# A two-layer hybrid backbone in fp32 pairs: where the vector work of the seven-product SwiGLU stands

## The chip, the cores and the metric

The kernel runs on one core of one Trainium2 chip. The metric is device microseconds for one execution of the whole program. TensorE (PE in the profile, with its weight loads as PEld) does the matmuls, VectorE (DVE), ScalarE (ACT) and GpSimd (POOL) do the element-wise work, and the SP queue issues nearly all transfers; GpSimd issues a few of its own.

## The reference

Two layers work on 512 latent tokens and 256 context tokens of width 1024. A layer is a half-weighted SwiGLU, a token mixer, and another half-weighted SwiGLU; each is modulated beforehand (shift, scale), gated, and closed by a LayerNorm.

```python
def swiglu(u, w_in, w_out):                 # w_in 1024 x 5632, w_out 2816 x 1024
    a, v = jnp.split(u @ w_in, 2, axis=-1)
    return (jax.nn.silu(a) * v) @ w_out

def ffn_sublayer(h, shift, scale, gate, w_in, w_out, g, b):
    y = swiglu(modulate(h, shift, scale), w_in, w_out)
    return layer_norm(ALPHA * h + FFN_RES * gate * y, g, b)
```

Mixer 0 is neighbourhood attention over a grid with all context keys beside it, mixer 1 a windowed attention with rotary positions and a sink. The shifts, scales and gates of a layer come from `silu(c) @ w_mod + b_mod`, one set for latent tokens and one for context tokens. Context tokens go through the same weights, except that the last layer drops them after its mixer has used them.

## The kernel before

Activations lie with the feature on the partitions: eight tiles of 128 x 768 (512 latent and 256 context tokens). Every product is made of fp32r pairs: a value is split into a high part and the rest, so one product is three matmuls (`mm3`, lines 145 to 148). Weights come in units of four raw quarters of 128 x 512. `split_w` (L102, L104) casts the high part on ScalarE and takes the rest on GpSimd; a variant (L106, L107) gets the rest from a transfer that GpSimd issues and that adds to what lies there. The pairs go into a ring of eight, or, on request, into the twelve "slab" tiles of the phase that the mixers use. Five raw buffers feed all of it.

There are four SwiGLU calls, named 0a, 0b, 1a and 1b in the tiles' names. `ffn` cuts the 2816 hidden columns into 11 chunks `ci` of 256, that is two blocks `i` of 128.

- An ordinary chunk: `av` makes the two products of a block for one group of tokens (48 matmuls into `pa` and `pv`), then silu, a multiplication, a cast to `gh` and the rest to `gl`. `down` multiplies with the output weights, six matmuls per output tile `pd`, and `accumulate` (L427) adds the gated result to the residual `z`.
- A seven-product chunk (0a from `ci` 3, 0b and 1a from `ci` 2, in each case to `ci` 8; none in 1b): `seven` computes the two products of a block with a Strassen-like scheme, seven products of 12 matmuls with 384 columns. `quarters` forms the four sums of weight quarters (`S`, L538: two on VectorE, two on GpSimd) and splits seven operands. `sums` formed the matching sums of activations once per call (`x`, `T`, L487 to L509), and `fourth` one more. The output sums (L567) add the seven results, in SBUF tiles `y`, and make `gh` and `gl`. The `down` of such a chunk is held back until the first `seven` of the next chunk has been emitted.

Beside that runs the modulation vector of later sub-layers: `gemv_dve` makes a list of steps, each a multiply-and-reduce on VectorE (L198, tile `jk`) of one transposed weight tile (`wt` in two buffers, or `zspare`, L195). `tick` emits steps at a pace that spreads them over the chunks, and `behind` keeps each step after the VectorE instruction that `last` names; it does not keep it ahead of anything. In 0a there are 192 steps, in 0b 96, in 1a 128, of which the last 64 use each weight tile once and all others twice.

The order on each engine is made by the Tile framework's planner from its own cost estimates, instruction by instruction, by program order where several are ready. Each engine then takes its list strictly in that order, and so does the SP queue.

In chunk 0 of 0b and 1b the LayerNorm of the last token groups is not finished when the chunk starts (`apart`, lines 665 to 672): the first group is computed and sent down, and then the chunk's three weight units are read, cast and split a second time for the remaining groups.

Of the kernel before, what the change touches and what calls it, by code (L numbers as in the profile page):

```python
# [8 lines left out]
F32 = mybir.dt.float32  # L9
# [29 lines left out]
def hybrid_kernel(ctx: ExitStack, tc: tile.TileContext, h0, cc, crow, wmod, wmodt, bmod, lnp, wst,  # L39
# [391 lines left out]
    def ffn(nm, groups, gt, mid, post, units=(), opened={}, head=None, apart=None):  # L431
# [7 lines left out]
        def av(w, f, g, gh, gl, ps=None, k0=0):  # L439
            c0, c1, st = g  # L440
            n = c1 - c0
            if ps:
                pa, pv = ps
            else:
                pa = bank("mm", f"pa{nm}_{f}_{c0}")
                mmk(pa[:, :n], w, 0, c0, c1, k0)
                pv = bank("c", f"pv{nm}_{f}_{c0}")
                mmk(pv[:, :n], w, P, c0, c1, k0)
            sl = t2(f"sl{nm}_{f}_{c0}", "sl")
            nc.scalar.activation(sl[:, :n], pa[:, :n], AF.Silu)  # L450
            nc.vector.tensor_tensor(out=sl[:, :n], in0=pv[:, :n], in1=sl[:, :n], op=ALU.mult)
            nc.scalar.copy(gh[:, c0:c1], sl[:, :n])
            nc.vector.tensor_tensor(out=gl[:, c0:c1], in0=sl[:, :n], in1=gh[:, c0:c1].bitcast(F32), op=ALU.subtract)

        turn = [0]

        def next_bank(nm):
            turn[0] += 1
            return bank(("mm", "s", "c")[turn[0] % 3], nm)

        def down(w, ci, gs, g, ticks):
            c0, c1, st = g
            for d in range(DT):
                pn = f"pd{nm}_{ci}_{c0}_{d}"
                pd = (next_bank(pn) if ticks else bank("sst"[d % 3], pn))[:, :c1 - c0]
                for i in range(2):
                    mm3(pd, rw(w, i, d * P, (d + 1) * P), [t[:, c0:c1] for t in gs[i]], i == 0, i == 1)
                accumulate(pd, d, c0, c1, st, gts[0])
                if ticks:
                    tick()  # L470

        gts = []
        nb = groups[-1][1] // 256
# [56 lines left out]
        def quarters(u):  # L530

            src = wst[u].rearrange("p (k c) -> p k c", c=256)
            a11, a12, a21, a22 = [raw_quarter(src[:, h * 4:h * 4 + 4, m * P:m * P + P], f"{u}_{m}{h}")
                                  for m in range(2) for h in range(2)]

            def tt(eng, n, a, b, o):
                t = t2(f"S{u}_{n}")
                eng.tensor_tensor(out=t[:], in0=a[:], in1=b[:], op=o)  # L538
                return t

            def pair(n, src):
                hi, lo = ring_pair(f"{u}_{n}")
                split_w(hi, lo, src)
                return hi, lo

            out = [pair("a11", a11), pair("a12", a12)]
            s1 = tt(nc.vector, 1, a21, a22, ALU.add)
            s2 = tt(nc.vector, 2, s1, a11, ALU.subtract)
            out += [pair("s2", s2), pair("s1", s1)]
            s4 = tt(nc.gpsimd, 4, a12, s2, ALU.subtract)  # L550
            s3 = tt(nc.gpsimd, 3, a11, a21, ALU.subtract)
            return out + [pair("s4", s4), pair("s3", s3), pair("a22", a22)]

        def seven(un, u, gh, gl):

            w = quarters(u)
            plain = [[[half(t[h4 * 4 + k], h) for t in (uh, ul)] for k in range(4)] for h4, h in ((0, 0), (1, 0), (1, 1), (0, 1))]
            b11, b21, b22, x4 = plain

            def product(n, b):  # L560
                ps = next_bank(f"p{n}{un}")
                for k in range(4):
                    mm3(as_half(ps[:, 0:n2]), [t[:, k * P:(k + 1) * P] for t in w[n]], b[k], k == 0, k == 3)
                return ps[:, 0:n2]

            def op(out, x, y, o=ALU.add, eng=nc.vector):
                i = eng.tensor_tensor(out=out, in0=x, in1=y, op=o)  # L567
                if eng is nc.vector:
                    last[0] = i
                return i  # L570
# [12 lines left out]
            tick()  # L583
            op(sb, product(4, b22), sb)
            nc.scalar.activation(sb, sb, AF.Silu)
            tick()
            op(va, product(5, ts[2]), va)
            op(vb, va, vb)
            tick()
            op(va, va, product(6, x4), ALU.subtract)  # L590
            for h, (v, x) in enumerate(((vb, sb), (va, sa))):
                op(v, v, x, ALU.mult)
                nc.scalar.copy(half(gh, 1 - h), as_half(v))
# [5 lines left out]
        gts.append(gt())  # L599
        late_downs = []  # L600
        s0 = NCH if nb == 2 else 3 if opened else 2
        weight = [0] + [2.2] * (s0 - 1) + [1.0] * (NCH - 2 - s0)
        each = sum(n + 1 for n, _ in bg) / (sum(weight) - 0.1)
        for ci in list(range(NCH)) + [("r", NCH - 2)]:
            r = isinstance(ci, tuple)
            if not r and 0 < ci < NCH - 2 and nb > 2:
                phase("T")
                pace[0] = each * weight[ci] / (2 * DT if ci < s0 else 2 * DT + 14)
                if ci == s0 - 1:
                    saved = sums()  # L610
            if not r and s0 <= ci < NCH - 2:
# [21 lines left out]
                continue  # L633
            if ci == NCH - 2:
                phase("S")
            i0 = wpos[0]
            late = ci == NCH - 2
            if late:
                again = i0
# [667 lines left out]
```

## Time and profile before

| | |
|---|---|
| Time, median of 3 runs | 2940.4 us (2936.29 to 2943.12) |
| The profiled execution | 2943.35 us |
| Its span | 2941.6 us |
| PE busy | 2759.2 us (94%) |
| VectorE busy | 1868.6 us (64%) |
| GpSimd busy | 1609.7 us (55%) |
| ScalarE busy | 1206.0 us (41%) |
| Transferred | 319.07 MB, mean 108 GB/s |

How to read it: a row of a group names line, engine, operation, output and inputs with buffer numbers left out, then busy time and the mean duration of one in nanoseconds, then the idle time of the engine ahead of them and what ended it. A row of waits gives the microseconds in total, the number of times and the longest. A row of a stretch of time gives the stretch, its length, and the busy time of PE, PEld, VectorE, ScalarE and GpSimd with the number of instructions, then the granted clock of TensorE, the share of the transfer engines' time that was used, and GB/s. A row of the timeline begins with start and duration in microseconds, and ends, in brackets, with the idle time ahead of it and what ended that.

### The profile page before, as it was taken

The numbers are of one execution on the slowest core, as the hardware profiler recorded it, in microseconds if no ns is written. First come the engines' busy times: TensorE is split into PE (matmuls) and PEld (weight loads), VectorE is DVE, ScalarE is ACT, GpSimd is POOL, SyncE is SP. The second block draws the span as 40 slices with busy tenths as digits, with TensorE's granted clock in tenths as the row PEclk, the third lists the DMA queues.
The fourth block names the chain that finished last, engine by engine and source line by source line (L and its number), as shares of the span: only waits on it lengthen the run. The fifth ranks groups of instructions, "written<-read, shape, count | busy, mean of one in ns | idle before, by whom it ended". The sixth has DMA issues, their size and how long they took to land. (4 is left out here: it accounts for less than half of the span.)

```text
span 2941.6 us, 48796 instructions
## 1 busy us (share of the span) xinstructions
PE 2759.2 (94%) x17626; PEld 2479.4 (84%) x17626; DVE 1868.6 (64%) x4024; ACT 1206.0 (41%) x2460; POOL 1609.7 (55%) x1410
## 2 busy tenths in 40 slices
PE   8999999989999978999999799999997999899997
PEld 5788888888888867898998688989886777799997
DVE  3698777385555687765664977675648667733335
ACT  4223433266445453343433423434335655523233
POOL 4646554465434567665645766565446544744453
PEclk9999999999999989999999999999999999899998
DMA  8456555232211222545452325556522111333332
GB/s 298 133 159 175 131 138 157 84 89 80 66 55 52 69 81 77 140 112 125 113 149 77 92 80 158 136 166 160 160 84 61 52 40 30 90 91 93 100 111 75
DMA packets 259443, 319.07 MB, mean 108 GB/s; under 512 B 28160, under 2 KB 140928, under 8 KB 258176
## 3 DMA queue, kind: packets, MB, share of 16 engines
q1 hardware_dynamic: 247392, 294.83, 33.7%
q0 software_dynamic: 11520, 20.98, 4.2%
q8 instruction: 139, 2.28, 0.3%
q14 instruction: 104, 0.85, 0.1%
q10 hardware_dynamic: 288, 0.14, 0.0%
HBM read 309.05 MB, written 11.20 MB: 109 GB/s over the span
## 5 line engine op out<-in xcount | busy, mean ns | idle before, releaser
L104 POOL TENSOR_TENSOR wl<-wr,wh 128x512 fp32r<-128x512 f32 x392 | 517.9, 1339 | 425.3 <-ACT wh L102 322.4
L102 ACT CAST wh<-wr 128x512 fp32r<-128x512 f32 x392 | 239.0, 619 | 256.6 <-DMA wr<-in_wst_dram 44.1
L104 POOL TENSOR_TENSOR wl_s<-S,wh_s 128x512 fp32r<-128x512 f32 x160 | 218.5, 1374 | 92.0 <-ACT wh_s L102 91.7
L102 ACT CAST wh_s<-S 128x512 fp32r<-128x512 f32 x160 | 97.3, 619 | 270.8 <-DVE S L538 49.5
L104 POOL TENSOR_TENSOR wl_a<-wr,wh_a 128x512 fp32r<-128x512 f32 x120 | 160.1, 1338 | 72.9 <-ACT wh_a L102 67.7
L198 DVE CUSTOM_DVE_ANT_0 jk<-wt,cb 128x512 f32<-128x512 f32 x278 | 185.4, 678 | 7.2 <-ACT cb L211 3.8
L538 POOL TENSOR_TENSOR S<-wr,S 128x512 f32<-128x512 f32 x40 | 52.7, 1317 | 157.2 <-DVE S L538 92.4
L427 DVE SCALAR_TENSOR_TENSOR z<-pd0b,gt,z 128x256 f32<-128x256 f32 (+1 forms) x176 | 99.4, 597 | 30.4 <-PE pd0b L148 30.4
L102 ACT CAST wh_a<-wr 128x512 fp32r<-128x512 f32 x120 | 74.5, 620 | 103.4 <-POOL wl_a L104 15.4
L427 DVE SCALAR_TENSOR_TENSOR z<-pd0a,gt,z 128x512 f32<-128x512 f32 (+1 forms) x168 | 98.7, 617 | 27.3 <-PE pd0a L148 27.3
L427 DVE SCALAR_TENSOR_TENSOR z<-pd1a,gt,z 128x512 f32<-128x512 f32 (+1 forms) x168 | 98.1, 616 | 26.2 <-PE pd1a L148 26.2
L427 DVE SCALAR_TENSOR_TENSOR z<-pd1b,gt,z 128x256 f32<-128x256 f32 x147 | 69.4, 481 | 71.3 <-PE pd1b L148 69.5
L761 POOL TENSOR_SCALAR p<-p,l 128x512 f32<-128x512 f32 x64 | 44.8, 701 | 119.0 <-DVE l L859 110.9
L538 DVE TENSOR_TENSOR S<-wr,wr 128x512 f32<-128x512 f32 x40 | 29.4, 735 | 112.8 <-DMA wr<-in_wst_dram 112.8
L198 DVE CUSTOM_DVE_ANT_0 jk<-zspare,cb 128x512 f32<-128x512 f32 x138 | 92.6, 678 | 7.0 <-DMA zspare<-in_wmodt_dram 6.1
L305 POOL TENSOR_SCALAR z<-z,ag_None,ab_None 128x256 f32<-128x256 f32 (+1 forms) x78 | 72.0, 931 | 38.8 <-DVE uh L291 29.9
L146 PE MATMUL pa1b<-uh,wh 128*128 128x256 f32 x320 | 91.3, 285 | 0.5 <-DVE uh L291 0.5
L148 PE MATMUL pa1b<-uh,wl 128*128 128x256 f32 x320 | 91.1, 285 | 0.0
L146 PE MATMUL pv1b<-uh,wh 128*128 128x256 f32 x320 | 91.1, 285 | 0.0
L147 PE MATMUL pa1b<-ul,wh 128*128 128x256 f32 x320 | 91.1, 285 | 0.0
L147 PE MATMUL pv1b<-ul,wh 128*128 128x256 f32 x320 | 90.9, 284 | 0.0
L148 PE MATMUL pv1b<-uh,wl 128*128 128x256 f32 x320 | 90.9, 284 | 0.0
(1406 smaller groups left out, 10711.5 us busy)
## 6 DMA issues: line engine op xcount, KB each, us to landing
wr<-in_wst_dram SPq DMA_DIRECT2D x552, 256.0 KB
wt<-in_wmodt_dram SPq DMA_DIRECT2D x160, 256.0 KB
zspare<-in_wmodt_dram SPq DMA_DIRECT2D x80, 256.0 KB
wr_0b<-in_wst_dram SPq DMA_DIRECT2D x41, 256.0 KB
wr_1b<-in_wst_dram SPq DMA_DIRECT2D x41, 256.0 KB
wr_2b<-in_wst_dram SPq DMA_DIRECT2D x41, 256.0 KB
wr_3b<-in_wst_dram SPq DMA_DIRECT2D x41, 256.0 KB
wm<-in_wmod_dram SPq DMA_DIRECT2D x8, 1024.0 KB
```

The lines of the kernel that those rows point to most:

```text
L102: nc.scalar.copy(hi[:], src[:])
L104: nc.gpsimd.tensor_tensor(out=lo[:], in0=src[:], in1=hi[:].bitcast(F32), op=ALU.subtract)
L146: nc.tensor.matmul(ps, a[0], b[0], start=first, stop=False)
L147: nc.tensor.matmul(ps, a[0], b[1], start=False, stop=False)
L148: nc.tensor.matmul(ps, a[1], b[0], start=False, stop=last)
L198: x = nc.vector.tensor_tensor_reduce(out=junk[:], in0=w[:], in1=cb[st], scale=1.0, scalar=0.0, op0=ALU.mult, op1=ALU.add, accum_out=acc[:, ...
L305: nc.gpsimd.tensor_scalar(out=zs, in0=zs, scalar1=prm[2][:, d:d + 1], scalar2=prm[3][:, d:d + 1], op0=ALU.mult, op1=ALU.add)
L427: last[0] = nc.vector.scalar_tensor_tensor(out=zt(d, c0, c1), in0=pd, scalar=gt[:, d, st:st + 1], in1=zt(d, c0, c1), op0=ALU.mult, op1=ALU ...
L538: eng.tensor_tensor(out=t[:], in0=a[:], in1=b[:], op=o)
L761: nc.gpsimd.tensor_scalar(out=p, in0=p, scalar1=r, scalar2=0.0, op0=ALU.mult, op1=ALU.add)
```

## The change

1. *Output sums.* In `av` the product is written back into the PSUM bank `pv`, and `gh` and `gl` are made from there. In `seven`, result 3 is added straight from its bank by VectorE (it had been copied by ScalarE and added by GpSimd), and the last additions, the multiplications and the rests are done in the banks of products 5 and 6. So each VectorE operation there has at least one operand in PSUM. The upper half is finished right behind product 5.
2. *Weight sums.* All four sums `S` are on GpSimd.
3. *Steps.* `tick` is no longer called in `down`. It is called once behind each `av` of the chunks between 0 and the first seven-product chunk (four times per chunk), and, as before, behind each product of `seven` (14 times per chunk). The paces follow: an early chunk has the weight 1.6 instead of 2.2. `av` now sets `last` too.
4. *Reloads.* In chunk 0 of 0b and 1b the third unit (the output weights) goes into slabs, the first two stay in the ring, and nothing is read again.

```diff
@@ av
-            nc.vector.tensor_tensor(out=sl[:, :n], in0=pv[:, :n], in1=sl[:, :n], op=ALU.mult)
-            nc.scalar.copy(gh[:, c0:c1], sl[:, :n])
-            nc.vector.tensor_tensor(out=gl[:, c0:c1], in0=sl[:, :n], in1=gh[:, c0:c1].bitcast(F32), op=ALU.subtract)
+            last[0] = nc.vector.tensor_tensor(out=pv[:, :n], in0=pv[:, :n], in1=sl[:, :n], op=ALU.mult)
+            nc.scalar.copy(gh[:, c0:c1], pv[:, :n])
+            nc.vector.tensor_tensor(out=gl[:, c0:c1], in0=pv[:, :n], in1=gh[:, c0:c1].bitcast(F32), op=ALU.subtract)
@@ down
                 accumulate(pd, d, c0, c1, st, gts[0])
-                if ticks:
-                    tick()
@@ quarters
-            s1 = tt(nc.vector, 1, a21, a22, ALU.add)
-            s2 = tt(nc.vector, 2, s1, a11, ALU.subtract)
+            s1 = tt(1, a21, a22, ALU.add)
+            s2 = tt(2, s1, a11, ALU.subtract)
@@ seven
+            def finish(v, x, h):
+                op(v, v, x, ALU.mult)
+                nc.scalar.copy(half(gh, h), as_half(v))
+                op(half(gl, h), as_half(v), half(gh, h).bitcast(F32), ALU.subtract)
...
-            nc.scalar.copy(vb, product(3, ts[0]))
-            op(sb, va, vb, eng=nc.gpsimd)
+            op(vb, product(3, ts[0]), va)
             tick()
-            op(sb, product(4, b22), sb)
+            op(sb, product(4, b22), vb)
             nc.scalar.activation(sb, sb, AF.Silu)
             tick()
-            op(va, product(5, ts[2]), va)
-            op(vb, va, vb)
+            x = product(5, ts[2])
+            op(va, x, va)
+            op(x, x, vb)
+            finish(x, sb, 1)
             tick()
-            op(va, va, product(6, x4), ALU.subtract)
-            for h, (v, x) in enumerate(((vb, sb), (va, sa))):
-                op(v, v, x, ALU.mult)
-                nc.scalar.copy(half(gh, 1 - h), as_half(v))
-                op(half(gl, 1 - h), as_half(v), half(gh, 1 - h).bitcast(F32), ALU.subtract)
+            x = product(6, x4)
+            op(x, va, x, ALU.subtract)
+            finish(x, sa, 0)
             tick()
@@ the chunks
-        weight = [0] + [2.2] * (s0 - 1) + [1.0] * (NCH - 2 - s0)
+        weight = [0] + [1.6] * (s0 - 1) + [1.0] * (NCH - 2 - s0)
...
-                pace[0] = each * weight[ci] / (2 * DT if ci < s0 else 2 * DT + 14)
+                pace[0] = each * weight[ci] / (4 if ci < s0 else 14)
...
-            w = [wunit(again=again + i) if r else unit(ci == NCH - 1 and i == 2) for i in range(3)]
+            w = [wunit(again=again + i) if r else unit(i == 2 and (ci == NCH - 1 or ci == 0 and apart is not None)) for i in range(3)]
...
                     av(w[i], f"{cn}_{i}", g, *gs[i], opened.get((i, g)) if ci == 0 else None, 4 if late else 0)
+                    if nb > 2 and not r and 0 < ci < s0:
+                        tick()
...
                 dn(head[0])
-                w = [wunit(again=i0 + i) for i in range(3)]
                 avs(*[(g, i) for g in head[1:] for i in range(2)])
```

More of the change, by code (lines that the diff above doesn't have):

```diff
@@ L459, in next_bank, with down @@
             return bank(("mm", "s", "c")[turn[0] % 3], nm)
-        def down(w, ci, gs, g, ticks):
+        def down(w, ci, gs, g, spread):
             c0, c1, st = g
@@ L464, in down @@
                 pn = f"pd{nm}_{ci}_{c0}_{d}"
-                pd = (next_bank(pn) if ticks else bank("sst"[d % 3], pn))[:, :c1 - c0]
+                pd = (next_bank(pn) if spread else bank("sst"[d % 3], pn))[:, :c1 - c0]
                 for i in range(2):
@@ L534, in quarters, with tt @@
                                   for m in range(2) for h in range(2)]
-            def tt(eng, n, a, b, o):
+            def tt(n, a, b, o):
                 t = t2(f"S{u}_{n}")
-                eng.tensor_tensor(out=t[:], in0=a[:], in1=b[:], op=o)
+                nc.gpsimd.tensor_tensor(out=t[:], in0=a[:], in1=b[:], op=o)
                 return t
@@ L546, in quarters @@
             out = [pair("a11", a11), pair("a12", a12)]
-            s1 = tt(nc.vector, 1, a21, a22, ALU.add)
-            s2 = tt(nc.vector, 2, s1, a11, ALU.subtract)
+            s1 = tt(1, a21, a22, ALU.add)
+            s2 = tt(2, s1, a11, ALU.subtract)
             out += [pair("s2", s2), pair("s1", s1)]
-            s4 = tt(nc.gpsimd, 4, a12, s2, ALU.subtract)
-            s3 = tt(nc.gpsimd, 3, a11, a21, ALU.subtract)
+            s4 = tt(4, a12, s2, ALU.subtract)
+            s3 = tt(3, a11, a21, ALU.subtract)
             return out + [pair("s4", s4), pair("s3", s3), pair("a22", a22)]
@@ L564, in product, with op @@
                 return ps[:, 0:n2]
[L566 to L570, printed above, removed]
+            def op(out, x, y, o=ALU.add):
+                last[0] = nc.vector.tensor_tensor(out=out, in0=x, in1=y, op=o)
+            def finish(v, x, h):
+                op(v, v, x, ALU.mult)
+                nc.scalar.copy(half(gh, h), as_half(v))
+                op(half(gl, h), as_half(v), half(gh, h).bitcast(F32), ALU.subtract)
             sa, sb = [t2(f"y{un}_{i}", "sl")[:, 0:n2] for i in range(2)]
@@ L635, in ffn @@
                 phase("S")
-            i0 = wpos[0]
             late = ci == NCH - 2
             if late:
-                again = i0
-            w = [wunit(again=again + i) if r else unit(ci == NCH - 1 and i == 2) for i in range(3)]
+                again = wpos[0]
+            w = [wunit(again=again + i) if r else unit(i == 2 and (ci == NCH - 1 or ci == 0 and apart is not None)) for i in range(3)]
             cn = f"r{ci[1]}" if r else f"{ci}"
```

## The prediction

> **What bounds the kernel now.** I read the page first, then the stretches of the seven-product chunks one by one, then who waits for whom there, then the order of single instructions.
>
> ```profile
> span 2941.6 us, 48796 instructions
> PE 2759.2 (94%) x17626; PEld 2479.4 (84%) x17626; DVE 1868.6 (64%) x4024; ACT 1206.0 (41%) x2460; POOL 1609.7 (55%) x1410
> ```
>
> The profiled run took 2943.35 us, 1.75 beyond its span and 3 above the median 2940.4. TensorE is the bound, so the change can only win time in which TensorE does not issue. Each row below runs from the first seven-product matmul of a SwiGLU (0a, 0b, 1a) to the first of its last such product group.
>
> ```profile
> 213.10:484.70 271.60, 254.68 (x1415) 235.64 (x1414) 212.65 (x466) 100.90 (x187) 159.64 (x130) 1.00 0.54 145
> 1194.50:1499.20 304.70, 296.50 (x1679) 280.91 (x1678) 195.96 (x413) 120.50 (x221) 187.34 (x154) 0.99 0.47 123
> 1760.30:2080.20 319.90, 303.19 (x1679) 283.15 (x1678) 219.66 (x479) 120.64 (x223) 188.17 (x154) 0.98 0.57 154
> ```
>
> A busy PE row overstates, because records overlap; start-to-start is the true price:
>
> ```profile
> 289.03 0.34 PE L147 MATMUL p20a<-T0a_3l,wh_s 128*128 128x384 f32 x1
> 290.07 0.34 PE L147 MATMUL p30a<-T0a_1l,wh_s 128*128 128x384 f32 x1
> 148.91 0.39 PE L147 MATMUL pd0a<-gl0a,wh 128*128 128x512 f32 x1
> 149.83 0.39 PE L148 MATMUL pd0a<-gh0a,wl 128*128 128x512 f32 x1
> 152.23 0.28 PE L147 MATMUL pd0a<-gl0a,wh 128*128 128x256 f32 x1
> 152.70 0.28 PE L148 MATMUL pd0a<-gh0a,wl 128*128 128x256 f32 x1
> ```
>
> Six steps make 1.04 us at 384 columns (0.173 each), four make 0.92 at 512 (0.23) and 0.47 at 256 (0.1175). A seven() is 84 matmuls, 14.6 us; a down() over both groups 48 x 0.23 + 48 x 0.1175 = 16.7 us; a chunk of two sevens and one down 45.8 us. The stretches hold 11, 13 and 13 sevens and 5, 6 and 6 downs: 243.7, 289.5 and 289.5 us, plus some 1.9 us each for the 11 matmuls above that count. What TensorE loses is thus about **26, 13 and 28.5 us, together 68**.
>
> ```profile
> PE pd0a L146 <- DVE z L427: 22.5, 28, 3.6
> PE pd1a L146 <- DVE z L427: 10.3, 20, 1.7
> PE pd1a L146 <- DVE y1a L567: 8.4, 3, 4.2
> PE pd0b L146 <- DVE z L427: 8.0, 13, 1.7
> ...
> DVE S L538 <- DMA wr<-in_wst_dram: 112.8, 19, 9.6
> DVE y0b L567 <- POOL y0b L567: 49.0, 13, 4.4
> ```
>
> TensorE waits in down() for banks that VectorE has not emptied, and VectorE itself stands waiting: for raw weights that a sum needs, and for a Pool addition inside seven(). One such chain:
>
> ```profile
> 313.27 0.69 DVE L538 TENSOR_TENSOR S<-wr,wr 128x512 f32<-128x512 f32 x1 [7.94 <-DMA wr<-in_wst_dram]
> 314.61 0.55 DVE L567 TENSOR_TENSOR y0a<-p40a,y0a 128x384 f32<-128x384 f32 x1
> 322.36 0.74 DVE L427 SCALAR_TENSOR_TENSOR z<-pd0a,gt,z 128x512 f32<-128x512 f32 x1
> ...
> 323.15 0.50 PE L146 MATMUL pd0a<-gh0a,wh_3b 128*128 128x512 f32 x1 [1.65 <-DVE z L427]
> ...
> 299.80:312.30 12.50, 12.50 (x74) 12.50 (x73) 4.39 (x11) 6.18 (x12) 5.45 (x6) 1.00 0.90 194
> 312.30:335.00 22.70, 19.11 (x99) 14.71 (x98) 21.45 (x40) 4.45 (x8) 13.12 (x10) 1.00 0.30 93
> ```
>
> VectorE's queue is in order: one sum waits 7.94 us for its transfer, products 4 to 6 stay in their banks, and the next down takes 22.7 us instead of 16.7. The price of that one wait is 6 us.
>
> **The change part by part.** Durations used:
>
> ```profile
> L567 DVE TENSOR_TENSOR y10a<-y00a,y10a 128x384 f32<-128x384 f32 x12 | 16.7, 1390 | 1.0
> L567 DVE TENSOR_TENSOR y00b<-p20b,y00b x14: 554/558/559, 1201.2 to 1504.1; 128x384 f32<-128x384 f32 x14
> L567 POOL TENSOR_TENSOR y0b<-y00b,y10b 128x384 f32<-128x384 f32 x14 | 14.8, 1057 | 0.0
> L538 DVE TENSOR_TENSOR S<-wr,wr 128x512 f32<-128x512 f32 x40 | 29.4, 735 | 112.8 <-DMA wr<-in_wst_dram 112.8
> L538 POOL TENSOR_TENSOR S<-wr,S 128x512 f32<-128x512 f32 x40 | 52.7, 1317 | 157.2 <-DVE S L538 92.4 <-issue 53.2 <-DMA cb<-in_crow_dram 6.5
> L198 DVE CUSTOM_DVE_ANT_0 jk<-wt,cb 128x512 f32<-128x512 f32 x278 | 185.4, 678 | 7.2 <-ACT cb L211 3.8 <-DMA wt<-in_wmodt_dram 2.8
> L107 POOL DMA_DIRECT2D wl_0b<-in_wst_dram x20 | 17.8, 892 | 39.6 <-ACT wl_0b L106 12.3 <-ACT gh0b L593 10.5 <-ACT gh1a L593 8.1
> ```
>
> *Sums with a PSUM operand.* Per seven, VectorE had ten operations, five of them with both inputs in SBUF, where the same shape averages up to 1.39 us instead of 0.558. It will have eleven at 0.558, 6.1 us. The Pool addition (1.06) and one ScalarE copy go; the wait of 49 us in 0b and its like in 0a and 1a have no cause left. Banks of products 5 and 6 and of pv are held 2 to 3 us longer; the next user of such a bank comes six products (12.5 us) or one av later, so I cost that at nothing; without that distance it would be 2 to 3 us per seven.
> The Trainium skill, page "SBUF — State Buffer", section "Who interferes with whom", says a VectorE instruction with two SBUF inputs is shut out while a GpSimd instruction reads SBUF. The 1.39 against 0.558 us agrees.
>
> *Weight sums on Pool.* VectorE loses 40 x 2 sums and the 112.8 us in which it stood for their transfers. Pool gains 80 x 1.32 us and loses 40 x 1.06, +1.6 us per seven; it works 11 x 1.32 = 14.5 us per seven and 4 x 0.89 for the transfers it issues, 32.6 of 45.8 us per chunk. Now Pool's head waits for raw weights; behind it stand the low parts (L104) and the accumulating transfers (L107), and TensorE after them. The lead:
>
> ```profile
> 318.87 3.15 POOL L104 TENSOR_TENSOR wl_s<-S,wh_s 128x512 fp32r<-128x512 f32 x2
> 339.13 0.33 PE L146 MATMUL p20a<-T0a_0h,wh_s 128*128 128x384 f32 x1
> ```
>
> The low part ends at 322.0 and is read at 339.1: 17 us. Two sums on Pool take 2.6 us of it, and TensorE's own 6 us of delay goes: 8 us remain. Cost zero; with the lead gone, 2.6 us per seven.
> The Trainium skill, page "GPSIMD Engine Reference", section "4.1 Engine selection", speaks against this part: an elementwise sum belongs on VectorE, GpSimd being about twice as slow. The two L538 rows agree (1317 against 735 ns); by that rule the change would lose, which is the second rival.
>
> *Steps beside products alone.* The 416 steps are the same in number. In 0a a seven-chunk gets 193/9.1 = 21.2 of them in 14 ticks instead of 18.7 in 30, so 10.6 per seven: 7.2 us, with 6.1 above 13.3 of 14.6. Then down() has only its accumulations:
>
> ```profile
> L427 DVE SCALAR_TENSOR_TENSOR z<-pd0a,gt,z 128x512 f32<-128x512 f32 x88 | 63.5, 743 | 24.0 <-PE pd0a L148 24.0
> L427 DVE SCALAR_TENSOR_TENSOR z<-pd0a,gt,z 128x256 f32<-128x256 f32 x80 | 35.5, 478 | 3.3 <-PE pd0a L148 3.3
> ...
> PE pd0a L146 <- DVE z L427: 3.4, 4, 1.5
> ```
>
> 8 x 0.743 + 8 x 0.478 = 9.8 of 16.7 us: VectorE has room to catch up. The last row is 180 to 240 us, the down of 0a's chunk 2, where steps stood between accumulations; with 0b's and 1a's chunk 1 I take 5 us back.
> The steps' transfers move too and meet the weights' (DMA share 0.90 above, raws waited for 8 us). Three tiles in flight with 8 us are some 5 per seven. 0a needs 5.3, 0b (11.4 steps per chunk, two per tile) 2.9, and 1a 3.8, but 7.7 once its last 64 steps use a tile each. There steps come late and VectorE stands for wt instead of wr. I leave a loss of 7 us in 0a, 4 in 0b and 12 in 1a; bounds are 0 and the 68 as now. **Gain: 68 - 23 = 45.**
>
> *Fewer reloads.* 24 transfers, casts and low parts go in 0b and 1b.
>
> ```profile
> 1080.00:1140.00 60.00, 46.17 (x308) 43.31 (x309) 56.48 (x103) 28.33 (x59) 50.23 (x44) 0.89 0.38 111
> L487 DVE TENSOR_TENSOR x0b<-x0b,ul 128x384 f32<-128x384 f32 x12 | 13.0, 1087 | 0.0
> L104 POOL TENSOR_TENSOR wl_0b<-wr_0b,wh_0b 128x512 fp32r<-128x512 f32 x21 | 28.2, 1343 | 23.2 <-PE pv1b L147 5.9 <-PE pv0b L147 4.0 <-PE pv0a L147 4.0
> ...
> 1156.48 0.28 PE L148 MATMUL pd0b<-gh0b,wl_3b 128*128 128x256 f32 x1
> 1150.00:1194.50 44.50, 43.17 (x262) 38.36 (x261) 28.91 (x54) 13.19 (x25) 23.17 (x18) 1.00 0.32 89
> ```
>
> In 0b's first chunk VectorE (56 of 60) and Pool (50) are full while PE is idle 14 us at a clock of 0.89. Twelve low parts (16 us of Pool) leave. But the sums of activations (x0b, T) move back: their T tiles now wait for the slabs that hold the down weights, which in today's times are read last at 1156.5. VectorE then still has its work of the 1150 row, and product 2 of the first seven reads T at 1199 (it ends at 1201.2, in the y00b<-p20b row above). The bounds are -17 (third rival) and +14, all that PE idles there; I take 4, as VectorE has 15 us free in that row. In 1b I take 1: the same low parts go, but no sums of activations stand there.
>
> Sum: 45 + 5 + 5 = 55. 2943.35 - 55 = 2888, and 3 less against the median: **2885**.
>
> **The rivals.** *The wait only moves to wt.* VectorE stands for step tiles as long as it stood for raws. For: DMA share 0.90. Against: jk waited 2.8 us for wt in all. The Pool-addition waits (8.4 and like rows) and the early 10 still come back: 2940 - 8 - 10 = 2922.
> *Pool's chain decides: slower.* Raw weights land later than the 8 us lead covers; every seven waits two Pool sums, less the addition: 40 x (2.6 - 1.06) = 62 us, the 45 does not come, 10 stay: 2940 + 62 - 10 = 2992. It decides from raws 8 us later than now. Against: no PE wait for wl_s or wh_s is among TensorE's waits.
> *Late sums in 0b.* All 32 operations (20 of L487, 12 lows) come behind 1156.5: 32 x 1.09 = 35 us, and 25 us of the 1150 row's other work between them, end at 1216 against 1199: 17 us lost and 4 not gained, 2906. Against: 10 of the 32 need no T tile, and Pool, which stretched them to 1.09, is freer.
> *Not what it says.* The steps are only held behind an instruction, not ahead of one, so the planner may still put them into downs. Then 1 to 2 us more remain per down, 20 downs: 2915.
>
> **How the numbers follow.** Forecast 2885 (2867 to 2900): 0.55. Late sums 0.15, steps in downs 0.11, wait moved 0.09, Pool 0.06, nothing measurable 0.04. The range 2860 to 2924 takes the first four and leaves some 0.15 out; its low end is the forecast with the 23 us of loss gone and 2 more. 0.2% (6 us) is about what a measurement can tell. Faster 0.90, same 0.04, slower 0.06.
>
> **What would show it.** Right: no VectorE wait for wr; the three stretches near 253, 295 and 303 us; jk between product operations; PE waits on L427 under 15 us; Pool's S waiting for wr with no PE wait for wl_s. Wrong: jk waiting tens of us for wt, PE waiting for wl_s, or the gap before 0b's first seven growing.

## The result

| | before | after |
|---|---|---|
| Time, median | 2941.76 us (2936.29 to 2947.68, 4 runs) | 2873.59 us (2861.81 to 2875.67, 4 runs) |
| Ratio, 95% interval | | 0.976 (0.9727 to 0.9792) |
| The profiled execution, its span | 2943.35, 2941.6 us | 2874.1, 2872.3 us |

The changed kernel is 2.4% faster by the ratio, 71 us of 2944 (the medians of the kernel before lie between 2942 and 2946 us in all rounds). The forecast was 2885, 11 us too slow and inside its range. How well its reasons hold is another matter.

The head of the page after. The number of matmuls is the same; TensorE's share rose by a point, VectorE lost 121 us of busy time, GpSimd gained 4.

```profile
PE 2737.3 (95%) x17626; PEld 2476.0 (86%) x17626; DVE 1747.1 (61%) x3984; ACT 1170.4 (41%) x2396; POOL 1613.8 (56%) x1426
```

The three stretches of the seven-product chunks after, columns as before (stretch, length, busy PE, PEld, VectorE, ScalarE, GpSimd, clock, transfer share, GB/s). They were 271.6, 304.7 and 319.9 us long:

```profile
213.00:466.40 253.40, 249.82 (x1422) 238.03 (x1421) 181.85 (x446) 96.60 (x177) 168.91 (x141) 0.99 0.56 152
1169.60:1459.50 289.90, 289.62 (x1668) 277.05 (x1667) 177.05 (x389) 113.56 (x207) 203.01 (x169) 1.00 0.48 126
1718.90:2015.40 296.50, 291.64 (x1674) 277.86 (x1673) 193.33 (x445) 114.63 (x209) 198.04 (x165) 1.00 0.58 163
```

They give back 18.2, 14.8 and 23.4 us, together 56.4 of the 69.3 us by which the span is shorter. (They hold 4764 matmuls instead of 4773, which is some 2 us of this at 0.173 us each.) The first product of 0b starts at 1169.6 instead of 1194.5: 18.2 come from 0a's stretch and 6.7 from what lies between. From the last seven of 0b to the first of 1a 1.7 us come, behind 1a's last seven 4.5.

The waits after, first TensorE's, then VectorE's and GpSimd's:

```profile
PE pd0a L146 <- DVE z L427: 7.4, 9, 2.5
...
PE pd1a L146 <- DVE z L427: 3.7, 4, 1.2
...
PE pd1a L146 <- DVE gl1a L565: 3.1, 3, 1.5
...
DVE jk L198 <- DMA wt<-in_wmodt_dram: 57.8, 22, 7.0
...
POOL S L536 <- DMA wr<-in_wst_dram: 121.1, 31, 7.6
```

TensorE's waits for VectorE's accumulations fell from 40.8 us (22.5 + 10.3 + 8.0) to about 11. VectorE no longer waits for raw weights nor for a GpSimd addition. It now waits 57.8 us for the step tiles `wt` (2.8 before), and GpSimd waits 121.1 us for raws, where VectorE had waited 112.8. Most of the waiting didn't vanish; it stands on other instructions.

### The profile page after: what moved, and what is told of

Read it like the earlier page. It is cut to its first block, busy times and chain, and to the rows that moved or that the text cites. A ratio compares the mean times of both kernels' runs of the same rounds, so it can differ in the third digit from the quotient of the medians.

```text
span 2872.3 us, 48553 instructions
## 1 busy us (share of the span) xinstructions
PE 2737.3 (95%) x17626; PEld 2476.0 (86%) x17626; DVE 1747.1 (61%) x3984; ACT 1170.4 (41%) x2396; POOL 1613.8 (56%) x1426
## 4 chain that ended last, share of the span: by engine, by line
PE 51%; DVE 9%; DMA 2%; issue 2%; ACT 2%; POOL 1%; DVEq 0%; SPq 0%; POOLq 0%; ACTq 0%
PE pd0b L146 2%; PE pd0b L147 2%; PE pd0b L148 2%; PE pd1a L146 2%; PE pd1a L147 2%; PE pd1a L148 2%; PE pa1b L146 1%; PE pa1b L148 1%; PE pa1b L147 1%; PE pv1b L146 1%; PE pv1b L147 1%; PE pv1b L148 1%; PE pd1b L146 1%; PE wo L753 1%; PE pd1b L148 1%
## 5 line engine op out<-in xcount | busy, mean ns | idle before, releaser
L104 POOL TENSOR_TENSOR wl<-wr,wh 128x512 fp32r<-128x512 f32 x392 | 512.0, 1325 | 447.6 <-ACT wh L102 330.6
L104 POOL TENSOR_TENSOR wl_s<-S,wh_s 128x512 fp32r<-128x512 f32 x160 | 210.7, 1353 | 53.5 <-ACT wh_s L102 53.1
L198 DVE CUSTOM_DVE_ANT_0 jk<-wt,cb 128x512 f32<-128x512 f32 x278 | 184.9, 679 | 59.5 <-DMA wt<-in_wmodt_dram 57.8
L536 POOL TENSOR_TENSOR S<-wr,wr 128x512 f32<-128x512 f32 x80 | 108.0, 1350 | 140.1 <-DMA wr<-in_wst_dram 121.1
L148 PE MATMUL pd1b<-gh1b,wl 128*128 128x256 f32 x336 | 93.3, 279 | 0.0
```

Source lines behind the costliest of these rows:

```text
L104: nc.gpsimd.tensor_tensor(out=lo[:], in0=src[:], in1=hi[:].bitcast(F32), op=ALU.subtract)
L148: nc.tensor.matmul(ps, a[1], b[0], start=False, stop=last)
L198: x = nc.vector.tensor_tensor_reduce(out=junk[:], in0=w[:], in1=cb[st], scale=1.0, scalar=0.0, op0=ALU.mult, op1=ALU.add, accum_out=acc[:, ...
L536: nc.gpsimd.tensor_tensor(out=t[:], in0=a[:], in1=b[:], op=o)
```

## The experiments

All ratios are against the kernel before, run on the same chip in turn. "Worth" is the distance of the ratio from 1, times 2944 us. Starts of a stretch's first and last product come from the instructions of the tiles p00a, p00b and p01a in each trace. Each stretch is that of one execution, and the order of matmuls isn't the same in every kernel, so a few can stand ahead of a stretch in one and inside it in another: the three hold 4757 to 4781 matmuls in the other kernels of the table, but 4731 with output sums alone and 4730 with old steps. At 0.173 us each that is some 7 and 6 us.

| kernel | median us | ratio (95%) | worth us | the three stretches us |
|---|---|---|---|---|
| after | 2873.6 | 0.976 (0.9727 to 0.9792) | +71 | 253.4, 289.9, 296.5 |
| output sums alone | 2907.8 | 0.9879 (0.9853 to 0.9905) | +36 | 260.2, 292.8, 303.2 |
| steps alone | 2924.1 | 0.9929 (0.9902 to 0.9956) | +21 | 254.5, 306.5, 311.0 |
| reloads alone | 2931.7 | 0.9954 (0.9938 to 0.997) | +14 | 270.3, 308.8, 317.2 |
| weight sums alone | 2990.5 | 1.0151 (1.0125 to 1.0177) | -44 | 283.0, 328.6, 333.3 |
| after, old output sums | 2946.8 | 1.0012 (0.9998 to 1.0025) | -4 | 274.0, 317.2, 318.4 |
| after, old weight sums | 2879.9 | 0.9783 (0.9763 to 0.9804) | +64 | 252.0, 292.1, 300.6 |
| after, old steps | 2869.5 | 0.9754 (0.9737 to 0.9771) | +72 | 255.0, 287.2, 291.6 |
| after, 0b's reloads back | 2875.5 | 0.9775 (0.9753 to 0.9798) | +66 | 251.4, 291.3, 293.2 |

**One part at a time.** Each kernel is the kernel before with one numbered part of the change, its lines as in the diff above.

Part 1, output sums in `av` and `seven`:

> The kernel before with part 1 alone (output sums with a PSUM operand, no GpSimd addition in a seven). Theory (VectorE's queue stands for others' work): the wait for the GpSimd addition goes, 103 us of it on VectorE before, the wait of the weight sums for raw weights (113 us) stays; TensorE's waits for y tiles go, those for accumulations stay in part: 2922 us, 15 to 25 less than before. Rival (it is the amount of VectorE work, stretched where both inputs are in SBUF): VectorE gets most of the relief here, some 45 us less, 2897.

Measured 2907.8, between the theory's 2922 and the rival's 2897. VectorE stands for raws as long as before, and still the three stretches are the shortest of the four kernels, 40 us less than before, of which some 7 are the 42 matmuls that stand outside:

```profile
DVE S L538 <- DMA wr<-in_wst_dram: 122.1, 33, 8.8
```

Part 2, weight sums on GpSimd:

> The kernel before with part 2 alone (all weight sums on GpSimd). Theory: VectorE no longer waits for raw weights, the wait for the GpSimd addition stays and may grow, since that addition now stands behind the weight sums in GpSimd's queue: 2917 us, 15 to 35 less. Rival (GpSimd's chain of sums and low parts decides): no gain, TensorE waits for wl_s, 2942 to 2992.

Measured 2990.5: 44 us slower. The theory fell outright. The rival's number is there, but not its mechanism: no TensorE wait for wl_s appears in the trace. VectorE's waits for raws are gone, and those for the GpSimd addition have grown from 49.0, 36.5 and 17.9 us to

```profile
POOL S L538 <- DMA wr<-in_wst_dram: 130.0, 35, 7.8
...
DVE y0b L567 <- POOL y0b L567: 84.7, 13, 13.0
DVE y1a L567 <- POOL y1a L567: 80.6, 11, 12.6
...
DVE y0a L567 <- POOL y0a L567: 66.4, 10, 11.6
```

One such chain in the timeline of that kernel (start, duration, instruction, idle time ahead of it and its releaser):

```profile
1346.46 0.56 DVE L567 TENSOR_TENSOR y00b<-p20b,y00b 128x384 f32<-128x384 f32 x1 [0.85 <-PE p20b L148]
...
1353.49 1.29 POOL L538 TENSOR_TENSOR S<-wr,wr 128x512 f32<-128x512 f32 x1 [6.30 <-DMA wr<-in_wst_dram]
...
1357.86 1.26 POOL L567 TENSOR_TENSOR y0b<-y00b,y10b 128x384 f32<-128x384 f32 x1
...
1359.16 0.56 DVE L567 TENSOR_TENSOR y0b<-p40b,y0b 128x384 f32<-128x384 f32 x1 [11.54 <-POOL y0b L567]
...
1360.08 1.52 POOL L538 TENSOR_TENSOR S<-wr,S 128x512 f32<-128x512 f32 x1
...
1360.28 5.42 DVE L567 TENSOR_TENSOR y10b<-y00b,y10b 128x384 f32<-128x384 f32 x1
...
1361.34 1.51 POOL L538 TENSOR_TENSOR S<-wr,wr 128x512 f32<-128x512 f32 x1
1362.60 2.68 POOL L104 TENSOR_TENSOR wl_s<-S,wh_s 128x512 fp32r<-128x512 f32 x2
...
1366.41 0.80 PE L146 MATMUL pd0b<-gh0b,wh_2b 128*128 128x512 f32 x1 [3.62 <-DVE y00b L567]
```

VectorE's part of what GpSimd is to add, y00b, is ready at 1347.0. The addition stands in GpSimd's order behind a weight sum that waits 6.30 us for its transfer, and runs at 1357.86; VectorE stands 11.54 us for it. Then a second thing shows: a VectorE addition with both operands in SBUF takes 5.42 us instead of 0.56. It starts while GpSimd works without a gap from 1360.08 to 1365.28, and ends 0.4 us after that. It isn't alone: of the 40 additions of this kind in that run 34 took over 0.6 us, and each of these began while a GpSimd instruction ran and ended 0.41 to 0.43 us behind the end of one. TensorE's down product waits for what follows.

Part 3, steps (no `tick` in `down`, one behind each early `av`, new paces):

> The kernel before with part 3 alone (steps beside products and behind av, none in down; av sets the mark the steps stand behind). Theory: both waits of VectorE stay, and the steps now stand in the stretch in which VectorE waits; the downs are free to catch up: 2932 us, 0 to 20 less. Rival (steps beside accumulations are what TensorE waits for): 45 less, 2897.

Measured 2924.1, better than the theory's 2932. 0a's stretch gains 17 us, 1a's 9, 0b's none (306.5 against 304.7). VectorE's waits for raws stay at 91.1 us, but those for the GpSimd addition fall from 103.4 us to 62.2 (28.1, 20.4 and 13.7): steps now run where VectorE would have stood.

Part 4, reloads:

> The kernel before with part 4 alone (no second reading of weights in the first chunk of 0b and 1b, output weights in slabs). Theory: 1b's first chunk wins some 4 us, 0b's wins in the first chunk and gives it back as the sums of activations come behind the slabs' last use: 2936 us, 3 to 9 less. Rival (late sums): 0b loses more than both win, 2945.

Measured 2931.7, better than either number and nearer the theory's. The four single worths sum to 36 + 21 + 14 - 44 = 27 us; together they are worth 71. So some 44 us come from parts acting on each other, far more than the intervals (4 to 10 us either way on one worth), and undoing shows which.

**One part taken back.** The changed kernel with the old output sums, the lines of `seven` (and `av`) as before:

```diff
-            op(vb, product(3, ts[0]), va)
+            nc.scalar.copy(vb, product(3, ts[0]))
+            op(sb, va, vb, eng=nc.gpsimd)
```

> Changed kernel with the output sums as before (GpSimd addition, ScalarE copy of product 3, multiplications from SBUF). In-order theory (weight sums on GpSimd hurt only while VectorE needs an addition queued behind them): the gain turns into a loss close to the weight sums' own alone, -14 and -14 of the other two on +45, so 2950 to 2965, VectorE waiting over 180 us for the addition. Rival (the parts add up, each worth what it was alone): the changed kernel plus 38, about 2912.

Measured 2946.8, just under the in-order theory's 2950 to 2965 and far from 2912. The whole gain is gone. VectorE stands for the addition again, 183.4 us with 0a's 28.7, and

```profile
DVE y0b L565 <- POOL y0b L565: 94.1, 14, 11.4
...
DVE y1a L565 <- POOL y1a L565: 60.6, 13, 10.4
```

With the other three parts in place the output sums are worth 74 us (from -4 to +71), alone 36.

The changed kernel with the first two weight sums on VectorE:

```diff
-            s1 = tt(1, a21, a22, ALU.add)
-            s2 = tt(2, s1, a11, ALU.subtract)
+            s1 = tt(nc.vector, 1, a21, a22, ALU.add)
+            s2 = tt(nc.vector, 2, s1, a11, ALU.subtract)
```

> Changed kernel with the first two weight sums of each seven back on VectorE. Theory (with the GpSimd addition out of the way the sums on GpSimd free VectorE from standing for raw weights): 2888 to 2900, VectorE waiting some 90 to 110 us for raw weights again and TensorE some 20 to 30 us more for banks of the down products. Rival (the other three parts give all of the gain, as their single effects -38, -22 and -14 add up to -74, and the weight sums on GpSimd are worth nothing): 2870 to 2878.

Measured 2879.9, between the two. The waits for raws are back, and TensorE hardly notices:

```profile
DVE S L536 <- DMA wr<-in_wst_dram: 87.7, 28, 7.1
...
PE pd0a L146 <- DVE z L427: 13.8, 12, 2.5
...
PE pd1a L146 <- DVE z L427: 7.3, 5, 2.7
```

The theory's 20 to 30 us of waits for banks came out as some 10 more than after. The weight sums on GpSimd are worth some 7 us of 71, and the intervals (0.9763 to 0.9804, 0.9727 to 0.9792) leave room for nothing at all.

The changed kernel with the steps in `down` and the paces of before:

> Changed kernel with the modulation steps back between the accumulations of down and the old paces. Theory (the steps crowd the down, where TensorE waits for banks): 2884 to 2892, with the waits of the down products for z back above 30 us together. Rival (once the sums are moved VectorE has room enough for the steps anywhere): 2871 to 2877.

Measured 2869.5, a little under the rival's window: the rival is right. The steps are worth 21 us alone and nothing beside the other parts. VectorE waits less for step tiles when they are spread. The stretches of 0b and 1a are 2.7 and 4.9 us shorter than after, but they also hold 14 and 18 fewer matmuls (1654 and 1656 against 1668 and 1674), some 2.4 and 3.1 us, so little of it is time that TensorE lost:

```profile
DVE jk L198 <- DMA wt<-in_wmodt_dram: 21.8, 13, 5.6
...
PE pd0a L146 <- DVE z L427: 11.1, 7, 3.8
```

The changed kernel with 0b's twelve weight tiles read a second time, 1b's not:

```diff
                 dn(head[0])
+                if nb > 2:
+                    w = [wunit(again=i0 + i) for i in range(3)]
```

> Changed kernel with 0b's twelve reloaded weight tiles back and 1b's left out. Theory of the prediction (the low parts that go are worth 4 us in 0b's first chunk, though the sums of activations wait longer): 2876 to 2880, the first seven-product matmul of 0b at 1172 to 1175 instead of 1169.6. Rival (with VectorE and GpSimd relieved by the other parts, the waiting sums of activations cost more than the low parts did): 2862 to 2870, first matmul before 1166.

Measured 2875.5, half a microsecond under the theory's window; first product of 0b at 1173.5 us, inside it. The whole time can't be told from the changed kernel's. The stretch from 0a's last seven to 0b's first says more. It is 709.8 us before, 718.3, 708.6, 711.0 and 711.9 in output sums alone, steps alone, weight sums alone and in this run; without the reloads 703.0 (reloads alone), 703.2 (after), 706.2 (old output sums) and 703.8 (old weight sums), and 711.1 with old steps. The runs further down fall in line: 711.0 with the reloads (only the addition gone), 704.2, 703.3 and 704.7 without. The medians are 711.0 and 704.0: some 7 us.

**What in the output sums pays.** The kernel before, with only the GpSimd addition taken out of VectorE's path; multiplications and rests stay in SBUF:

```diff
-            nc.scalar.copy(vb, product(3, ts[0]))
-            op(sb, va, vb, eng=nc.gpsimd)
+            op(vb, product(3, ts[0]), va)
...
-            op(va, product(5, ts[2]), va)
-            op(vb, va, vb)
+            x5 = product(5, ts[2])
+            op(va, x5, va)
+            op(vb, x5, vb)
```

> Kernel before; of the output sums only the one GpSimd addition goes: product 3 is added by VectorE straight from PSUM and product 5 is added to both sums; the multiplications and low parts keep both inputs in SBUF. In-order theory (the addition stands on GpSimd behind weight sums that wait for transfers, and VectorE stands for it): most of the 38 us of part 1 alone come here, time 2910 to 2918, no VectorE wait for a GpSimd addition. Port theory (part 1 pays because five operations per seven no longer have two SBUF inputs): at most 10 us come, 2936 or more.

Measured 2920.75, ratio 0.9924 (0.9904 to 0.9944): 22 of part 1's 36 us, some 60%, just outside the in-order theory's window. The other 13 or so come with the rest of part 1: the PSUM operands in `seven` and `av`, and the upper half that is finished right behind product 5. No run takes these apart. The groups of VectorE's multiplications in this kernel, in the changed kernel the same operations (mean ns behind the busy time):

```profile
L567 DVE TENSOR_TENSOR y00b<-y00b,y0b 128x384 f32<-128x384 f32 x14 | 14.3, 1020 | 0.1
```

```profile
L565 DVE TENSOR_TENSOR p50b<-p50b,y0b 128x384 f32<-128x384 f32 x14 | 7.9, 567 | 1.5
```

**How near GpSimd is to being the bound.** The changed kernel with each of the four weight sums issued twice, its output unchanged:

```diff
-                nc.gpsimd.tensor_tensor(out=t[:], in0=a[:], in1=b[:], op=o)
+                for _ in range(2):
+                    nc.gpsimd.tensor_tensor(out=t[:], in0=a[:], in1=b[:], op=o)
```

> Changed kernel with each of the four weight sums of a seven issued twice on GpSimd, the output is the same; 4 x 1.33 us more GpSimd work per seven, in a chunk about 43 of 45.8 us. Theory of the prediction (a lead of about 8 us between a low part and its use, which 5.3 us do not exhaust): at most 10 us slower than the changed kernel, 2874 to 2884, hardly a TensorE wait for the weights' low parts. Rival (GpSimd's chain already decides): the doubled sums show one by one, 37 x 2 to 37 x 5.3, 2945 to 3070, with TensorE waiting for wl_s.

Measured 2944.1, ratio 1.0 (0.9988 to 1.0013): 71 us slower than the changed kernel, a little under the rival's window of 2945 to 3070 and far from the theory's. GpSimd has 198 us more work (1812.2 against 1613.8), so over a third of it shows, 1.9 us per seven. The room wasn't there: in the changed kernel's three stretches GpSimd is busy for 570 us and stands 118 for raws, 688 of 840, and 198 more don't fit; with the doubled sums it is 761 and 93 of 908. A piece of the timeline of the run with doubled sums, then waits over 1188 to 1507 us:

```profile
1321.36 2.54 POOL L104 TENSOR_TENSOR wl_s<-S,wh_s 128x512 fp32r<-128x512 f32 x2
...
1322.70 0.45 PE L148 MATMUL p20b<-T0b_0h,wl_s 128*128 128x384 f32 x1 [0.44 <-POOL wl_s L104]
...
1337.12 0.50 PE L148 MATMUL pd0b<-gh0b,wl_0b 128*128 128x512 f32 x1 [2.74 <-DMA wl_0b<-in_wst_dram]
```

```profile
PE pd0b L148 <- DMA wl_0b<-in_wst_dram: 10.5, 6, 2.7
...
ACT wh_s L102 <- POOL S L537: 135.1, 38, 9.9
...
DVE y0b L566 <- ACT y00b L575: 34.0, 7, 5.7
```

TensorE takes some of the low parts as they come (4.9 us of waits for wl_s in all), and it waits for the accumulating transfers that GpSimd issues late. ScalarE passes the delay on: its copy of result 0 stands behind casts that wait for sums, and VectorE behind that copy.

**Two versions built on these readings.** The sums of activations issued behind the products of the last early chunk:

```diff
-                if ci == s0 - 1:
-                    saved = sums()
...
                 avs(*([(g, i) for g in head for i in range(2)] if ci == 0 else [(a, 0), (b, 0), (a, 1), (b, 1)]))
+                if nb > 2 and ci == s0 - 1:
+                    saved = sums()
```

> Changed kernel with the sums of activations issued behind the SwiGLU products of the last chunk ahead of the sevens instead of ahead of them (0b and 1a). Theory (they stand in VectorE's queue ahead of the hidden rows' low parts, for which the down products waited 3.4 and 2.1 us at 1143 to 1155): 4 to 8 us faster than the changed kernel, 2865 to 2870. Rival (the sums then end so late that the first seven waits for them): 2874 to 2885, and the idle time moves to the start of the first seven.

Measured 2869.45, ratio 0.9752 (0.9731 to 0.9773): inside the theory's window, but not told apart from the changed kernel. What it aimed at is in the changed kernel's timeline:

```profile
1143.56 0.74 PE L146 MATMUL pd0b<-gh0b,wh 128*128 128x512 f32 x2 [2.11 <-ACT gh0b L452]
...
1155.00 0.79 PE L146 MATMUL pd0b<-gh0b,wh 128*128 128x512 f32 x1 [3.39 <-DVE gl0b L453]
```

0b's first product comes at 1164.7 instead of 1169.6, but stretches differ by as much from one execution to the next: 0a's, the same code in after, in 0b's reloads back and here, took 253.4, 251.4 and 249.3 us.

The same with the steps spread over the down products in the seven-product chunks only:

```diff
-                pace[0] = each * weight[ci] / (4 if ci < s0 else 14)
+                pace[0] = each * weight[ci] / (4 if ci < s0 else 2 * DT + 14)
...
-                        down(w, f"{ci}", gs, g, True)
+                        down(w, f"{ci}", gs, g, True, True)
```

> Changed kernel with the sums of activations late, as before this run, and with the modulation steps split: in the first chunks beside the products as in the changed kernel, in the seven-product chunks spread over the down products too, at the paces of before. Theory (the steps in the downs were worth nothing to move, but bunching them makes VectorE wait 58 us for their tiles, and the stretches of 0b and 1a were 3 and 5 us shorter with them spread, while 0b's first seven began 8 us later with them in the first downs): about 8 us below late_sums' neighbours, 2860 to 2866, the wait of jk for wt under 20 us. Rival (TensorE's residual in the sevens is set elsewhere and both placings are equal): 2868 to 2874.

Measured 2868.35, ratio 0.9736 (0.9723 to 0.975), at the near edge of the rival's window. The wait for step tiles fell to 18.8 us, as expected. The stretches are 247.5, 289.2 and 294.1 us, 9 us shorter than after with the same number of matmuls, but only 2.4 us shorter than with late sums alone (249.3, 290.6 and 293.3). The 3 and 5 us on which the theory counted were mostly the matmuls that stood outside. It is the fastest of all, by some 7 us against the changed kernel's ratio; the two intervals still overlap (0.9727 to 0.975), so that it beats the changed kernel is likely, not shown.

## Why the prediction was right, and where it was not

*The sum.* Forecast 55 us, measured 71. The frame held: count what TensorE loses in the three stretches and ask what of it comes back. The stretches gave 56.4 us where 45 were forecast, the rest 12.9 where 10 were. By the forecast's own price for the matmuls that stand in the stretches after (246.8, 289.5 and 290.5 us) the loss left is 6.6, 0.4 and 6.0 us, not 7, 4 and 12. That residual is the term that was mis-sized: 13 for 23. That the total came so near although the parts were priced wrongly, as the next paragraph shows, is partly luck: most of the loss came back, whichever part brought it.

*Which part earns it.* Here the prediction was wrong. It read the 112.8 us in which VectorE stood for raws as the main loss, and priced the GpSimd addition by TensorE's rows for it, 8 us, in the rival "the wait only moves to wt". The runs turn this round. With the addition gone, 87.7 us of standing for raws cost about 7 us of time (old weight sums); with the addition there, moving the raws' wait away cost 44 (weight sums alone). The step that failed is "the Pool-addition waits (8.4 and like rows)", 8 us: taking the addition alone out of the path measured 22, and the whole of part 1 74 beside the others. Within the three stretches before there were more rows of that kind than the one of 8.4 us,

```profile
PE pd0a L146 <- DVE y0a L567: 2.7, 1, 2.7
...
PE pd0b L146 <- DVE y0b L567: 4.9, 2, 3.3
```

and with the small ones 16.9 us; without the addition all rows for such sums come to 2.9, while the waits for z stay (24.2 and 24.0). The rest of the 22 doesn't stand under waits at all: between these two kernels, whose stretches hold 4773 and 4775 matmuls, the stretches became 20.7 us shorter, 14.1 of it idle time of TensorE and 6.6 busy time (854.4 to 847.8). The granted clock shows where the busy time went:

```profile
1812.65 0.79 PE L146 MATMUL pd1a<-gh1a,wh_1b 128*128 128x512 f32 x1 [4.25 <-DVE y1a L567]
1813.24 0.63 PE L147 MATMUL pd1a<-gl1a,wh_1b 128*128 128x512 f32 x1
...
1812.60:1819.00 6.40, 6.35 (x15) 4.99 (x16) 6.29 (x12) 1.55 (x3) 3.43 (x3) 0.51 0.39 117
```

After that wait the clock is 0.51 for 6.4 us, and matmuls of 512 columns come 0.43 us apart instead of 0.23. The same stands behind two more waits for such sums in these stretches (3.29 us at 1245.9 and 2.64 us at 2013.5, the clock 0.51 for 3.5 and 3.4 us). Together that is 13.3 us at half clock, some 6.5 us lost; with the addition gone the clock is 1.00 in all three stretches. So a long wait here cost more than itself. What decides whether the clock falls isn't shown: in 0a, with a 2.7 us wait for y0a, it is 1.00 throughout.

Between before and after it is 33.1 us idle and 23.3 busy. Of the busy part the clock explains some 3 us and the nine matmuls some 2. Some 7 more are a matter of the records: a matmul's row lasts 0.39 us where the next can start after 0.23, so the first 0.16 us of a wait counts as busy, and 54 waits became 8. The rest isn't split here; the first matmul behind a wait often takes longer too (0.50 to 0.80 us in the rows shown). So rows of waits named 14 of 21 us and 32 of 56.

*Weight sums at no cost.* True in the changed kernel, and only there. The rival "Pool's chain decides" was given 2992 and 0.06; weight sums alone landed on 2990.5, but by an addition that waited in GpSimd's order, not by low parts that came late. So that agreement is no confirmation. The lead of some 8 us held. In the changed kernel the low parts of one block's four sums, with the first use of the first and of the third:

```profile
1308.14 2.80 POOL L104 TENSOR_TENSOR wl_s<-S,wh_s 128x512 fp32r<-128x512 f32 x2
...
1317.82 2.55 POOL L104 TENSOR_TENSOR wl_s<-S,wh_s 128x512 fp32r<-128x512 f32 x2
...
1324.81 0.34 PE L148 MATMUL p20b<-T0b_0h,wl_s 128*128 128x384 f32 x1
...
1328.97 0.34 PE L148 MATMUL p40b<-uh,wl_s 128*128 128x384 f32 x1
```

The first two, for products 2 and 3, end by 1310.9 and are read from 1324.8 on, 14 us later; the other two, for products 4 and 5, end by 1320.4 and are read from 1329.0 on, 8.6 us later. Counted in order over all 160 such low parts, the shortest lead is 5.8 us and the middle one for each product 11 to 13. What the doubled sums met was not this lead but the room on GpSimd: 570 us busy and 118 standing, of 840.

The Trainium skill, page "GPSIMD Engine Reference", section "4.1 Engine selection", puts elementwise sums on VectorE, GpSimd being about twice as slow. For the weight sums alone its advice agrees with the measurement (44 us lost), though the trace shows the queued addition as the way in which they were lost. In the changed kernel, where nothing of VectorE's is queued behind them, putting two of them back on VectorE gained nothing (2879.9 against 2873.6).

*Operands in PSUM, and banks held longer.* The first is right: the multiplications take 567 ns (795 before, 1020 with only the addition gone). The second, banks of products 5 and 6 held longer at a cost of nothing, failed where VectorE comes late. In 0a of the changed kernel:

```profile
257.99 0.69 DVE L198 CUSTOM_DVE_ANT_0 jk<-wt,cb 128x512 f32<-128x512 f32 x1 [6.27 <-DMA wt<-in_wmodt_dram]
...
265.58 0.56 DVE L565 TENSOR_TENSOR gl0a<-p50a,gh0a 128x384 fp32r<-128x384 f32 x1 [2.07 <-ACT gh0a L569]
...
266.19 0.51 PE L146 MATMUL pd0a<-gh0a,wh_2b 128*128 128x512 f32 x1 [3.00 <-DVE gl0a L565]
```

VectorE stands 6.27 us for a step tile, then 2.07 us for ScalarE, and so reads product 5's bank for the last time at 265.58. `next_bank` goes round six banks, so the fifth output tile of the `down` behind a seven gets that bank, and TensorE waits 3.00 us for it. Three like waits stand in 1a, 3.1 us together, at the same output tile, behind waits of 5.3 to 7.0 us for step tiles. In 0a the granted clock was then 0.51 for 6.9 us (267.5 to 274.4), some 3.4 us more. That makes some 9.5 of the 13 us that TensorE still loses. With the steps spread over the `down` products too (the last version above) the waits of this kind are 0.4 us.
The 5.42 us row fits the Trainium skill, page "SBUF — State Buffer", section "Who interferes with whom", better than any in the prediction: a VectorE instruction with two SBUF inputs is shut out while GpSimd reads SBUF. Here it was shut out through four GpSimd instructions in a row.

*Steps.* Moved as said: in the three stretches 96 of 316 steps stood directly between two accumulations of `down` before, 1 of 293 after. The rival that they stay in the downs fell. But "jk waiting tens of us for wt" was listed as a sign that the change fails; it came (57.8 us), and what of it reached TensorE is the 9.5 us above. That is the loss of which the prediction left 7 us in 0a, 4 in 0b and 12 in 1a ("VectorE stands for wt instead of wr"): right in kind, and in 0a in size; in 0b and 1a too large. The 5 us from early chunks did not come in 0a (first product at 213.1 before, 213.0 after). In its windows before

```profile
120.00:147.90 27.90, 23.05 (x131) 19.96 (x131) 23.00 (x32) 9.30 (x18) 26.87 (x20) 0.94 0.59 198
147.90:213.10 65.20, 61.74 (x356) 53.30 (x355) 59.24 (x147) 14.11 (x27) 24.40 (x18) 1.00 0.51 152
```

and after

```profile
120.00:147.90 27.90, 23.01 (x122) 20.34 (x120) 25.75 (x46) 9.22 (x19) 25.54 (x19) 0.82 0.60 201
147.90:213.00 65.10, 64.20 (x367) 55.98 (x367) 59.56 (x160) 13.86 (x27) 28.91 (x23) 1.00 0.60 184
```

the idle time of the second window did fall, from 3.5 to 0.9 us, but nine fewer matmuls were done in the first, at a granted clock of 0.82 instead of 0.94 (half clock for some 10 us instead of some 3), and they had to follow. Why the clock was lower there is open.

*Reloads.* 4 us in 0b and 1 in 1b were forecast; the stretch ahead of 0b's first seven shows some 7, and behind 1a's last seven 4.5 us came, 4.0 of it from 1b's first product on (410.2 to 406.2 us to the end). Both terms were too small. The rival "late sums" has its mark (the 3.39 and 2.11 us waits at 1143 to 1155), a fraction of the 17 us it was given.

*Open.* Why the steps are worth 21 us alone and nothing beside the rest was not tested. It fits the traces that alone they fill time in which VectorE stands for the GpSimd addition (103.4 to 62.2 us), that with the addition gone there is none to fill, and that bunched they hold product 5's bank. Whether the weight sums are worth anything in the end (7 us, the intervals overlap) these runs can't tell. Nor is it known what in the 13 us of part 1 beyond the addition pays.

## What to carry to other kernels

Price a set of waits by what the bound engine loses, not row by row: the rows name the last releaser, they leave out a lower clock behind a long wait, and here parts worth 36, 21, 14 and -44 us alone were worth 71 together. Before work that waits for transfers moves to another engine's in-order queue, list what of the critical path is queued there, and take that out first. Where a VectorE operation with both inputs in SBUF runs beside GpSimd, try it with one operand in PSUM. And before calling a bank that is held longer free, ask how late its last reader can come: here one that was late by 8 us used up the distance to the next user.

## What was not expected of the hardware

- One VectorE addition of 128 x 384 with both operands in SBUF took up to 5.45 us where its neighbours take 0.56, while GpSimd worked without a gap beside it. Its group with weight sums alone (mean 2452 ns, before 939; second row minimum, median and maximum):

```profile
L567 DVE TENSOR_TENSOR y10b<-y00b,y10b 128x384 f32<-128x384 f32 x14 | 34.3, 2452 | 1.5
...
L567 DVE TENSOR_TENSOR y10b<-y00b,y10b x14: 559/1603/5452, 1222.4 to 1546.5; 128x384 f32<-128x384 f32 x14
```

- Behind three waits of TensorE of 2.6 to 4.3 us in the kernel before the granted clock was 0.51 for 3.4 to 6.4 us, which lost some 6.5 us more than the waits themselves.
- VectorE may stand 86 us for transfers inside stretches of 845 us in all at a cost of some 7 us, but 198 us more of GpSimd work cost 71, though GpSimd was at 56% of the span (68% of the three stretches, 82% with its waits for raws).
